# Expert lookups row by row, query products on unsplit weights, in a fused two-block kernel

## The chip, the cores and the metric

The kernel runs on one core of one Trainium2 chip. The metric is the device time of one execution in microseconds (us). One execution was also taken by the hardware profiler; its rows are used below. The engines are PE (TensorE: matmuls), DVE (VectorE), ACT (ScalarE), POOL (GpSimd) and SP (SyncE, which only issues transfers). Each runs its own instructions in program order and waits for the others by semaphores.

## What is computed

Two transformer blocks follow one another on 256 tokens of width 1024, in f32. The change lies in the second half of the first block, a layer that looks up experts (PEER), and at its border to the second block:

```python
h2 = modulate(x, norm_ffn_g, shift2, scale2)           # rmsnorm, scale, shift
q = (h2 @ w_q).reshape(T, 8, 2, 128)                   # 8 heads, two halves each
s = einsum('thpn', q, sub_keys)                        # 2 x 128 key scores
sv, si = top_k(s, 16)                                  # per half
cv, ci = top_k(all 16 x 16 sums of sv, 16)             # 16 of them
expert = si[half 0] * 128 + si[half 1] at ci           # 16 of 16384 experts
g = softmax(cv)
a = gelu(einsum('cd,chkd->chk', h2, u_tab[expert]))    # one row of 1024 each
y = einsum('chk,chkd->cd', g * a, v_tab[expert])
x = rmsnorm(x + gate2 * y, norm_final_g)               # then the second block
```

So each token takes 8 x 16 = 128 rows of `u_tab` and as many of `v_tab`, 4 KB each: 2 x 256 x 128 x 4 KB = 268 MB, all of it gathered from HBM by index.

## The kernel before

Tokens are worked on in two tiles of 128, one token to a partition. One gather (`gather`, L801) takes one expert row for each of the 128 tokens of a tile, 128 x 4 KB; `k` counts the 16 experts of one head. A unit is a tile and a head, 16 units in all, 8 of the first tile and then 8 of the second. For an expert row, DVE forms the dot product of `u` with the token's `h2` (L905, one value for each token, into a column of `act`). ACT applies Gelu (L930), DVE multiplies by the softmax weight (L931), ACT makes a diagonal matrix `dg` of the 128 weights (L916), and PE multiplies `dg` with `v` in two matmuls of 512 columns that add up in `acc` over the 128 rows of a tile (L919).

The loop (L869 to L937) goes by half units of eight rows. In half unit n it gathers and dots the u rows of this half and gathers and accumulates the v rows of the half before, one of each in turn; Gelu and weights come once for eight rows, behind the half. After the last half unit a round follows with eight v rows and no u rows. Each kind has three buffers of two rows (E, H, I for u; A, G, J for v). POOL issues every gather. Scores, top-k and the finish of the first tile are cut into steps (`Steps`, L88) that the loop runs between the rows: `more_queries` makes the queries and scores of heads 1 to 7, `next_topk` the expert numbers of the unit behind, `finish_tile` (L812) adds `x` and normalises, and its result is split for the second block.

Weight blocks (128 x 1024 f32) come through `Weights` (L28): a ring of seven raw buffers, and for blocks with `do_split` an ACT copy `hi` (L53) and a DVE difference `lo` (L54) in six buffers each. A product with such weights is three matmuls (`mm3`, L139 to L141) of hi and lo parts. The query weights `wq` are 16 blocks, two to a head. Four pairs of them are loaded into big buffers G, K, J, I ahead of time (`place`, L219), the others through the ring; all are split. The activations of the queries are split too (`xah`, `xal`, L635 and L638), scaled by A2 and still without the row's norm; the norm `rs` is multiplied into the product (L671) and the shift part `cq` added (L672). Before the loop stand the last output projection in four column blocks j (L625 to L640), head 0's queries for both tiles (L842 to L849), and the first steps of the first top-k; then six u gathers are issued (L859).

After the loop `band_values` (L948) starts the second block: its first products with `w_in_2`, for tile 0 between the finish steps of tile 1 and for tile 1 behind them.

## Time and profile before

| what | value |
|---|---|
| time, median of 3 runs | 1245.27 us (1242.26 to 1246.87) |
| profiled execution | 1246.47 us; span of its instructions 1244.7 us |
| PE busy | 1064.2 us, 86% of the span |
| DVE busy | 845.4 us, 68% |
| ACT busy | 462.0 us, 37% |
| POOL busy | 536.0 us, 43% |
| DMA | 390.59 MB, mean 314 GB/s |
| mean granted clock of TensorE | 0.983 |

Busy shares are means over stages with different limits. The page cuts the span into forty slices of 31 us and gives for each the busy tenths of the engines and of the DMA engines and the GB/s that they moved. The gathers run from about 222 to 890 us, slices 8 to 28. In these the DMA row reads 9 throughout and GB/s mostly 407 to 409, while PE reads 7 or 8. Before and behind them PE reads 9 nearly everywhere and DMA less.

### The profile page before, as it was taken

Reading aid. Unit: us, or ns where it says so; the run is one execution under the profiler, and the core shown is the slowest. Engines: PE = TensorE matmul, PEld = TensorE weight load, DVE = VectorE, ACT = ScalarE, POOL = GpSimd, SP = SyncE. Lnnn points to the kernel's source line nnn. Section 1 sums busy time; section 2 is a strip of 40 time slices with the busy share of each in tenths; the row PEclk is TensorE's granted clock in tenths of the full one; section 3 lists DMA queues with packets and bytes.
Section 4 is the critical chain, followed back from the end, with each engine's and each line's share of the span. In section 5 each row is a group of like instructions: output and inputs, shape, how many; then the busy total and the mean of one; then the engine's idle time right before and its main releaser. Section 6 shows DMA issues by size and latency. Waiting matters only on the chain.

```text
span 1244.7 us, 15745 instructions
## 1 busy us (share of the span) xinstructions
PE 1064.2 (86%) x5328; PEld 707.2 (57%) x5328; DVE 845.4 (68%) x1846; ACT 462.0 (37%) x887; POOL 536.0 (43%) x569
## 2 busy tenths in 40 slices
...
GB/s 346 330 315 307 321 284 153 278 346 406 409 386 392 407 408 409 409 409 409 358 409 409 409 409 409 409 409 409 347 289 185 153 186 123 197 181 194 183 123 34
DMA packets 161104, 390.59 MB, mean 314 GB/s; under 512 B 12472, under 2 KB 83648, under 8 KB 160768
## 3 DMA queue, kind: packets, MB, share of 16 engines
...
q10 hardware_dynamic: 640, 0.98, 0.2%
q14 instruction: 37, 0.30, 0.1%
HBM read 388.22 MB, written 1.06 MB: 313 GB/s over the span
## 4 chain that ended last, share of the span: by engine, by line
PE 37%; DMA 27%; DVE 12%; POOL 9%; issue 9%; ACT 4%; SPq 0%; DVEq 0%; POOLq 0%; ACTq 0%
DMA urows<-in_peer_u_dram,ex 19%; PE mm L139 7%; PE mm L141 7%; PE mm L140 7%; DMA vrows<-in_peer_v_dram,ex 5%; POOL vrows L806 5%; DVE dot L905 5%; POOL urows L806 5%; PE acc L919 3%; PE down L141 2%; PE down L139 2%; PE down L140 2%; DVE lo L54 1%; PE mp L407 1%; ACT hi L53 1%
## 5 line engine op out<-in xcount | busy, mean ns | idle before, releaser
L919 PE MATMUL acc<-vrows,dg 128*128 128x512 f32 x1024 | 491.5, 612 | 127.9 <-ACT dg L916 89.6
L905 DVE SCALAR_TENSOR_TENSOR dot<-urows,h2rows 128x1024 f32<-128x1024 f32 x256 | 312.0, 1219 | 173.7 <-DMA urows<-in_peer_u_dram,ex 172.3
L919 PEld LDWEIGHTS acc<-vrows,dg 128*128 128x128 f32 x1024 | 178.8, 190 | 420.7 <-issue 228.6
L806 POOL DMA_INDIRECT vrows<-in_peer_v_dram,ex x256 | 242.6, 948 | 103.8 <-issue 60.5
L806 POOL DMA_INDIRECT urows<-in_peer_u_dram,ex x256 | 241.7, 944 | 93.2 <-issue 65.4
L54 DVE TENSOR_TENSOR lo<-raw,hi 128x1024 fp32r<-128x1024 f32 (+1 forms) x152 | 182.0, 1222 | 89.6 <-ACT hi L53 88.0
L916 ACT ACTIVATE dg<-ident,wgt 128x128 f32<-128x128 f32 x256 | 96.0, 397 | 252.2 <-PE acc L919 246.7
L53 ACT CAST hi<-raw 128x1024 fp32r<-128x1024 f32 (+1 forms) x152 | 154.0, 1045 | 34.1 <-DMA raw<-in_w_in_dram 25.8
L139 PE MATMUL mm<-xh,hi 128*128 128x256 f32 x480 | 137.0, 285 | 2.2 <-ACT vab L1021 2.2
L140 PE MATMUL mm<-xl,hi 128*128 128x256 f32 x480 | 136.7, 285 | 0.0
L141 PE MATMUL mm<-xh,lo 128*128 128x256 f32 x480 | 135.6, 283 | 0.0
L139 PEld LDWEIGHTS mm<-xh,hi 128*128 128x128 f32 x480 | 91.1, 190 | 5.1 <-ACT vab L1021 2.5
L140 PEld LDWEIGHTS mm<-xl,hi 128*128 128x128 f32 x480 | 91.1, 190 | 0.4
L141 PEld LDWEIGHTS mm<-xh,lo 128*128 128x128 f32 x480 | 91.3, 190 | 0.0
L1120 POOL TENSOR_TENSOR r<-r,ln 128x512 f32<-128x512 f32 x2 | 3.0, 1488 | 195.2 <-ACT r L1119 195.2
L1176 DVE SCALAR_TENSOR_TENSOR u<-mm,col,u 128x255 f32<-128x255 f32 x88 | 42.4, 482 | 33.7 <-ACT u L1173 32.1
L337 POOL TENSOR_SCALAR p<-p,mnsm 128x128 f32<-128x128 f32 (+1 forms) x24 | 20.2, 851 | 91.1 <-DVE mnsm L335 79.2
L139 PE MATMUL mm<-hh,hi 128*128 128x256 f32 x160 | 47.6, 298 | 5.2 <-ACT hi L53 5.2
L852 POOL TENSOR_TENSOR h2T<-xT,rs 128x1024 f32<-128x1024 f32 x2 | 4.7, 2352 | 107.2 <-ACT rs L847 107.2
L1173 ACT ACTIVATE u<-mm,col 128x256 f32<-128x256 f32 x44 | 24.9, 566 | 59.1 <-PE mm L141 32.4
L141 PE MATMUL mm<-hh,lo 128*128 128x256 f32 x160 | 46.3, 289 | 0.5 <-DVE lo L54 0.5
L930 ACT ACTIVATE wgt<-act 128x8 f32<-128x8 f32 x32 | 6.6, 208 | 106.8 <-DVE dot L905 106.7
...
## 6 DMA issues: line engine op xcount, KB each, us to landing
...
urows<-in_peer_u_dram,ex POOLq DMA_INDIRECT x256, 8.0
```

Source lines behind the costliest of these rows:

```text
L53: self.nc.scalar.copy(hi, raw)
L54: self.nc.vector.tensor_tensor(lo, raw, hi.bitcast(F32), op=OP.subtract)
L139: nc.tensor.matmul(o, lh, rh, start=first, stop=False)
L140: nc.tensor.matmul(o, lh, rl, start=False, stop=False)
L141: nc.tensor.matmul(o, ll, rh, start=False, stop=last)
L337: eng.tensor_scalar(neg[:, s], neg[:, s], sm[:, i:i + 1], None, op0=OP.mult)
L806: nc.gpsimd.indirect_dma_start(out=g, out_offset=None, in_=tables[kind], in_offset=bass.IndirectOffsetOnAxis(ap=experts[unit][:, k:k + 1], ...
L905: nc.vector.scalar_tensor_tensor(dot, u, 1.0, h2rows, op0=OP.mult, op1=OP.mult, accum_out=act[:, half * HK + k:half * HK + k + 1])
L916: nc.scalar.activation(dg, ident, AF.Copy, scale=wgts[prev][:, k:k + 1])
L919: nc.tensor.matmul(acc[:, s], dg, v[:, s], start=prev == ((prev[0][0], 0), 0) and k == 0, stop=prev == ((prev[0][0], NH - 1), 1) and k == ...
L1173: nc.scalar.activation(dst, src, AF.Identity, bias=ccol[:, 3, c + f:c + f + 1], scale=ccol[:, 2, c + f:c + f + 1])
L1176: nc.vector.scalar_tensor_tensor(dst[:, n:], src[:, :256 - n], ccol[:, 2 - n, c + f:c + f + 1], dst[:, n:], op0=OP.mult, op1=OP.add)
```

## The change

Three things change together.

First, the query weights are no longer split. A query product is one f32 matmul (the chip works on it in four passes) with the raw block and with `xa`, a single f32 activation whose column 0 is the shift. All sixteen blocks are requested before the loop: seven through the ring, seven into the then unused `hi` and `lo` buffers (`borrow`), two into K.

Second, head 0 is done by token tile: `first_queries` makes tile 0's queries and scores alone, and tile 1's queries of head 0 come as the last of `more_queries`. Top-k of unit 0 reads the scores where PE left them.

Third, the loop goes row by row. A slot of 8 KB holds u and v of one expert row. There are seven slots for rows 0 to 111, and six from row 112 on, since D then serves the second block. In row s come the dot, Gelu, weight and `dg` of row s (`weigh`, three ACT instructions on one column, the last one the 128 x 128 diagonal), then PE's accumulation of row s - 1, then the gathers of u and v of row s + 6 (s + 5 from row 112 on). The finish of tile 0 runs every second row from row 129 on. Behind the loop, splits of `w_in_2` and products of `band_values` are interleaved with the finish of tile 1 in smaller parts.

```diff
+    def borrow(self, i, tag):
+        self.place(i, self.pool.tile([128, 1056], F32, tag=tag, name="whole", bufs=self.split_ahead))
...
-    def cols(key, w, c0, n):
...
-        cols(("wq", j), a["peer_wq"][0], j * 256, 256)
+        cols(("wq", j), a["peer_wq"][0], j * 256, 256, False)
     in2_order = [2568, 2824, 1544, 2056, 1800, 2312, 1280, 256, 768, 0, 512, 1024]
...
-    WQ_SLOTS = {"G": 4, "K": 14, "J": 6, "I": 2}
+    WQ_RING, WQ_K = 7, 14
     IN_SLOTS = {'A': [(0, 0), (0, 1)]}
-    ws.elsewhere = {wq_blocks[first + n] for first in WQ_SLOTS.values() for n in range(2)}
+    ws.elsewhere = set(wq_blocks[WQ_RING:])
     ws.elsewhere |= {W["in", j][g] for slot_blocks in IN_SLOTS.values() for j, g in slot_blocks}
...
             m.append(t)
         nc.vector.tensor_tensor(m[0], m[0], m[1], op=OP.add)
         split(mh[:, 2 * j:2 * j + 2, :], ml[:, 2 * j:2 * j + 2, :], m[0])
-        if j in (0, 2):
-            place("GK"[j // 2])
...
+    xa = big.tile([128, KC, 258], F32, tag="C", name="xa")
+    nc.vector.tensor_copy(xa[:, :, 0], shift2)
     sq_ps = aux_tile("sq_ps2")
     for j in range(4):
...
-            place("JI"[j])
         if j:
...
                                            modc[:, 16 + dc:17 + dc], xT[:, dc, :], op0=OP.mult, op1=OP.add)
-            nc.scalar.activation(xah[:, dc, 0:256], xT[:, dc, :], AF.Copy, scale=A2[:, dc:dc + 1])
...
         for dc in (2 * j, 2 * j + 1):
             nc.scalar.activation(sq2[:, dc, :], xT[:, dc, :], AF.Square)
-            nc.vector.scalar_tensor_tensor(xal[:, dc, 0:256], xT[:, dc, :], A2[:, dc:dc + 1],
-                                           xah[:, dc, 0:256].bitcast(F32),
-                                           op0=OP.mult, op1=OP.subtract)
+    for i in range(WQ_RING, WQ_K):
+        ws.borrow(wq_blocks[i], ("hi", "lo")[i % 2])
...
+    wq = {}
+    def wq_of(h):
+        if h not in wq:
+            wq[h] = [ws.get(i, 1) for i in W["wq", h]]
+        return wq[h]
+    def product(h, f, o, kcs, cs):
+        for kc in kcs:
+            nc.tensor.matmul(o, wq_of(h)[kc // 4][:, kc % 4, f * 128:(f + 1) * 128], xa[:, kc, cs],
+                             start=kc == 0, stop=kc == KC - 1)
...
+    cq0 = kp.tile([128, 2], F32, name="cq0", bufs=1)
+    def first_queries():
+        o = [mm_tile()[:, 0:129] for _ in range(2)]
+        for f in range(2):
+            product(0, f, o[f], range(0, 6), slice(0, 129))
+        square_sums(sq_ps, sq2, (6, 7))
+        for f in range(2):
+            product(0, f, o[f], (6, 7), slice(0, 129))
+        nc.scalar.copy(rs, rstd_rows(sq_ps, rstd))
+        qv = kp.tile([128, 512], F32, tag="qv", name="qv", bufs=1)
+        for f in range(2):
+            q = qv[:, f * 128:(f + 1) * 128]
+            nc.scalar.copy(cq0[:, f:f + 1], o[f][:, 0:1])
+            nc.vector.tensor_tensor(q, o[f][:, 1:129], rs[:, 0:128], op=OP.mult)
+            nc.vector.tensor_scalar(q, q, cq0[:, f:f + 1], None, op0=OP.add)
+        sp = aux_tile("sp")[:, 0:256]
+        key_scores(sp, 0, qv, 1, 128)
+        scores["first"] = sp.rearrange("p (a b) -> p a b", a=2)
...
     def queries(h):
...
+        n = 256 if h else 128
+        cs = slice(0, 257) if h else slice(129, 257)
+        o = [mm_tile()[:, 0:cs.stop - cs.start] for _ in range(2)]
+        for f in range(2):
+            product(h, f, o[f], range(0, KC // 2), cs)
+            if h:
+                yield
+            product(h, f, o[f], range(KC // 2, KC), cs)
+            yield
+        cq = kp.tile([128, 2], F32, tag="cq", name="cq") if h else cq0
         qv = kp.tile([128, 512], F32, tag="qv", name="qv", bufs=1)
...
+        for f in range(2):
+            q = qv[:, f * n:(f + 1) * n]
+            if h:
+                nc.scalar.copy(cq[:, f:f + 1], o[f][:, 0:1])
+            nc.vector.tensor_tensor(q, o[f][:, -n:], rs[:, 256 - n:], op=OP.mult)
             nc.scalar.activation(q, q, AF.Identity, bias=cq[:, f:f + 1])
...
+        sp = aux_tile("sp")[:, 0:2 * n]
+        key_scores(sp, h, qv, n // 128, n)
...
         scores[h] = kp.tile([128, 4, 128], F32, tag="scores", name="scores", bufs=8)
...
+        nc.scalar.copy(scores[h][:, 4 - n // 64:], sp.rearrange("p (a b) -> p a b", b=128))
         yield
...
-    def gather(kind, unit, k):
-        if k % 2 == 0:
...
-        g = rows[kind][:, k % 2, :]
...
+    row_tags = ["E", "H", "A", "I", "G", "J", "D"]
+    units = [(t, h) for t in range(2) for h in range(NH)]
+    N_ROWS = len(units) * K
+    SEVEN = 7 * K
+    rows = {}
...
+    def gather(s):
+        unit, k = units[s // K], s % K
+        r = slot(row_tags[s % 7 if s < SEVEN else (s - SEVEN) % 6], "uvrows")
+        for n, table in enumerate((a["peer_u"][0], a["peer_v"][0])):
+            nc.gpsimd.indirect_dma_start(out=r[:, n * 1024:(n + 1) * 1024], out_offset=None, in_=table,
+                                         in_offset=bass.IndirectOffsetOnAxis(ap=experts[unit][:, k:k + 1], axis=0))
+        rows[s] = r
...
+    first_queries()
...
-    ahead = [gather("u", (0, 0), k) for k in range(6)]
+    N_FIRST = 7
+    for s in range(N_FIRST):
+        gather(s)
...
+    more_queries = Steps(*(queries(h) for h in (*range(1, NH), 0)))
+    finish = Steps()
+    acc, dgs = None, {}
...
+        unit, k = units[s // K], s % K
+        c = slice(k, k + 1)
+        nc.scalar.activation(ge[:, c], act[:, c], AF.Gelu)
+        nc.scalar.activation(wgt[:, c], ge[:, c], AF.Copy, scale=gsm[unit][:, c])
+        dgs[s] = kp.tile([128, 128], F32, tag="dg", name="dg", bufs=3)
+        nc.scalar.activation(dgs[s], ident, AF.Copy, scale=wgt[:, c])
...
+    def accumulate(s):
+        t = units[s // K][0]
+        dg, v = dgs.pop(s), rows.pop(s)[:, 1024:2048]
+        for c in range(2):
+            cs = slice(c * 512, (c + 1) * 512)
+            nc.tensor.matmul(acc[:, cs], dg, v[:, cs], start=s % (N_ROWS // 2) == 0, stop=s % (N_ROWS // 2) == N_ROWS // 2 - 1)
+    next_row = N_FIRST
+    for s in range(N_ROWS):
+        n, k = s // K, s % K
...
+        if s == 6:
+            next_topk = Steps(topk(0, 1))
+        if n == 7 and k == 0:
+            more_queries.drain()
...
-        for k in range(HK):
-            if run:
-                u = ahead.pop(0) if ahead else gather("u", unit, half * HK + k)
-            if prev:
-                v = gather("v", prev[0], prev[1] * HK + k)
-            if run:
-                nc.vector.scalar_tensor_tensor(dot, u, 1.0, h2rows, op0=OP.mult, op1=OP.mult,
...
-                dg = kp.tile([128, 128], F32, tag="dg", name="dg", bufs=3)
-                nc.scalar.activation(dg, ident, AF.Copy, scale=wgts[prev][:, k:k + 1])
-                for c in range(2):
-                    s = slice(c * 512, (c + 1) * 512)
-                    nc.tensor.matmul(acc[:, s], dg, v[:, s], start=prev == ((prev[0][0], 0), 0) and k == 0,
-                                     stop=prev == ((prev[0][0], NH - 1), 1) and k == HK - 1)
-        if not run:
...
+        if s == N_ROWS // 2:
+            h2rows = h2rows_1
+        nc.vector.scalar_tensor_tensor(dot, rows[s][:, 0:1024], 1.0, h2rows, op0=OP.mult, op1=OP.mult,
+                                       accum_out=act[:, k:k + 1])
+        if s < 12 or k % 2:
+            more_queries.run()
+        next_topk.run(2 if n == 0 else 1)
+        if k % 2:
+            finish.run()
+        weigh(s)
+        if s:
+            if s - 1 in (0, N_ROWS // 2):
+                acc = pp.tile([128, 1024], F32, tag=("acc", "h2")[units[(s - 1) // K][0]], name="acc")
+            accumulate(s - 1)
+            if s == N_ROWS // 2:
+                xh, xl = slot3("C", "xh", KC, F32R), slot3("D", "xl", KC, F32R)
+                finish = Steps(finish_tile(0, acc))
+        if k == K - 5:
+            next_topk.drain()
+        last = next_row
+        while next_row < min(s + (7 if next_row < SEVEN else 6), N_ROWS):
+            gather(next_row)
+            next_row += 1
+        if last < next_row == N_ROWS:
             ws.limit, ws.queue = len(blocks), nc.gpsimd
             ws.prefetch()
             ws.queue = nc.sync
...
+    nc.scalar.activation(warm, eps_t[:, 0:1], AF.Sqrt)
+    accumulate(N_ROWS - 1)
...
-    ws.ensure(first_in2, first_in2 + 4)
...
...
+    def band_values(t, n, g):
...
     finish = Steps(finish_tile(1, acc))
     finish.run(2)
-    band_values(0)
+    ws.ensure(first_in2, first_in2 + 3)
+    for n, g in ((0, 0), (0, 1), (1, 0)):
+        band_values(0, n, g)
+    finish.run(2)
+    ws.ensure(first_in2, first_in2 + 4)
     finish.drain()
+    band_values(0, 1, 1)
     ws.ensure(first_in2, first_in2 + 6)
-    band_values(1)
+    for n in range(2):
+        for g in range(2):
+            band_values(1, n, g)
+            ws.parts.pop(vb_blocks[n][g])
```

How POOL's gathers stand against each other at the start of the loop, before (the last of the first six u gathers, then the loop; `ex` is the table of expert numbers, DMASW marks a gather done, DMAHW a plain transfer):

```order
L806 DMA urows_2401<-in_peer_u_dram,ex_2378 128x1024 [waits DMAHW5_49,DMAHW4_49]
L806 DMA urows_2401<-in_peer_u_dram,ex_2378 128x1024
L806 DMA urows_2503<-in_peer_u_dram,ex_2378 128x1024 [waits DMASW5_49,DMASW4_49,DVE_49]
L806 DMA urows_2503<-in_peer_u_dram,ex_2378 128x1024
L806 DMA urows_2585<-in_peer_u_dram,ex_2378 128x1024 [waits DMASW7_49,DMASW6_49,DVE_49]
L806 DMA vrows_2587<-in_peer_v_dram,ex_2378 128x1024 [waits DMAHW2_49]
L806 DMA urows_2585<-in_peer_u_dram,ex_2378 128x1024
L806 DMA vrows_2587<-in_peer_v_dram,ex_2378 128x1024
L806 DMA urows_2621<-in_peer_u_dram,ex_2378 128x1024 [waits DMASW1_49,DMASW0_49,DVE_49]
```

And now (the last of the first fourteen, then the loop):

```order
L826 DMA uvrows_2345<-in_peer_u_dram,ex_2313 128x1024 [waits DMASW6_49]
L826 DMA uvrows_2345<-in_peer_v_dram,ex_2313 128x1024 [waits DMASW7_49]
L826 DMA uvrows_2348<-in_peer_u_dram,ex_2313 128x1024 [waits DMASW0_49]
L826 DMA uvrows_2348<-in_peer_v_dram,ex_2313 128x1024 [waits DMASW1_49]
L826 DMA uvrows_2406<-in_peer_u_dram,ex_2313 128x1024 [waits DMASW2_49,DVE_49,PE_49]
L826 DMA uvrows_2406<-in_peer_v_dram,ex_2313 128x1024 [waits DMASW3_49]
L826 DMA uvrows_2420<-in_peer_u_dram,ex_2313 128x1024 [waits DMASW4_49,DVE_49,PE_49]
L826 DMA uvrows_2420<-in_peer_v_dram,ex_2313 128x1024 [waits DMASW5_49]
```

Before, u and v alternate, each with its own buffer, and a u buffer waits for DVE's dot. Now a row's u and v stand together, the u gather waits for DVE and PE, the v gather only for the transfer eight before it.

On DVE, from the last output projection (L633 before, L628 now) to the first top-k instruction, before:

```order
L54 TENSOR_TENSOR lo<-wqI,hi 128x1024 [waits DMAHW5_49,Activation_49]
L54 TENSOR_TENSOR lo<-wqG,hi 128x1024 [waits PE_49,Activation_49]
L633 SCALAR_TENSOR_TENSOR xT<-mm,modc,xT 128x256 [waits PE_49]
L633 SCALAR_TENSOR_TENSOR xT<-mm,modc,xT 128x256
L638 SCALAR_TENSOR_TENSOR xal<-xT,A_1961,xah 128x256 [waits Activation_49] x2
L313 RECIPROCAL rstd<-rstd 128x2 [waits Activation_49]
L671 TENSOR_TENSOR qv<-aux,rs 128x256 [waits Activation_49,Pool_49]
L671 TENSOR_TENSOR qv<-mm,rs 128x256 [waits Activation_49]
L703 MAX sv<-sp 128x8 [waits Activation_49]
```

And now:

```order
L628 SCALAR_TENSOR_TENSOR xT<-mm,modc,xT 128x256 [waits PE_49]
L628 SCALAR_TENSOR_TENSOR xT<-mm,modc,xT 128x256
L310 RECIPROCAL rstd<-rstd 128x2 [waits Activation_49]
L685 TENSOR_TENSOR qv<-mm,rs 128x128 [waits DVE_49,PE_49,Activation_49]
L686 TENSOR_SCALAR qv<-qv,cq_2244 128x128 [waits DVE_49]
L685 TENSOR_TENSOR qv<-mm,rs 128x128 [waits PE_49,Activation_49]
L686 TENSOR_SCALAR qv<-qv,cq_2244 128x128 [waits DVE_49]
L721 MAX sv<-sp 128x8 [waits PE_49]
```

The two lo splits ahead of the eviction, the lo part of the activations and the 256-column query steps are gone; four 128-column steps stand in front of top-k, and top-k waits for PE where it waited for ACT.

On DVE, from the last dot to the normalising of the second tile, before:

```order
L905 SCALAR_TENSOR_TENSOR dot,act<-urows,h2rows_4214 128x1024 [waits DMASW2_49,DVE_49]
L931 TENSOR_TENSOR wgt<-wgt,g 128x8 [waits Activation_49]
L54 TENSOR_TENSOR lo<-raw,hi 128x1024 [waits DMASW4_49,Activation_49]
L54 TENSOR_TENSOR lo<-raw,hi 128x1024 [waits DMASW5_49,Activation_49]
L819 TENSOR_TENSOR y_peer<-acc,gates 128x512 [waits PE_49]
L820 TENSOR_TENSOR y_peer<-y_peer,aux 128x512 [waits DVE_49,PE_49]
L819 TENSOR_TENSOR y_peer<-acc,gates 128x512
L820 TENSOR_TENSOR y_peer<-y_peer,aux 128x512 [waits DVE_49,PE_49]
L823 TENSOR_TENSOR st<-st 128x1 [waits Activation_49]
```

And now:

```order
L927 SCALAR_TENSOR_TENSOR dot,act<-uvrows,h2rows_4164 128x1024 [waits DMASW2_49,DVE_49]
L839 TENSOR_TENSOR y_peer<-acc,gates 128x512 [waits PE_49]
L840 TENSOR_TENSOR y_peer<-y_peer,aux 128x512 [waits DVE_49,PE_49]
L839 TENSOR_TENSOR y_peer<-acc,gates 128x512
L840 TENSOR_TENSOR y_peer<-y_peer,aux 128x512 [waits DVE_49,PE_49]
L54 TENSOR_TENSOR lo<-raw,hi 128x1024 [waits DMASW4_49,Activation_49]
L843 TENSOR_TENSOR st<-st 128x1
L846 RECIPROCAL st<-st 128x1 [waits Activation_49]
L849 SCALAR_TENSOR_TENSOR xin<-y_peer,st,gates 128x512 [waits DVE_49]
L849 SCALAR_TENSOR_TENSOR xin<-y_peer,st,gates 128x512
L54 TENSOR_TENSOR lo<-raw,hi 128x1024 [waits DMAHW1_49,DMASW5_49,Activation_49]
```

Before, the weights of eight rows and two lo splits of `w_in_2` stood between the last dot and `y_peer`. Now `y_peer` follows the last dot, one lo split stands between it and the sum `st`, and a second behind the normalised `xin`.

## Rows read from the trace of the kernel before

**Rows 1.** Busy us of each engine by stretch, granted clock, DMA rate.

```profile
core 0: us, PE busy (x) PEld busy (x) DVE busy (x) ACT busy (x) POOL busy (x), PEclk, DMA share, GB/s
218.00:230.00 12.00, 10.91 (x56) 8.76 (x56) 10.45 (x47) 5.35 (x13) 6.46 (x7) 0.72 0.44 137
230.00:270.00 40.00, 29.62 (x108) 18.95 (x109) 33.48 (x91) 13.78 (x27) 25.58 (x27) 0.83 0.91 341
340.00:400.00 60.00, 53.82 (x191) 29.02 (x190) 41.92 (x104) 19.11 (x42) 43.55 (x45) 1.00 1.00 388
560.00:640.00 80.00, 60.74 (x138) 23.24 (x136) 59.35 (x160) 21.39 (x49) 55.82 (x60) 0.98 0.99 389
640.00:880.00 240.00, 181.91 (x373) 63.76 (x372) 158.79 (x413) 52.25 (x125) 175.77 (x188) 0.99 1.03 409
218.00:890.00 672.00, 533.51 (x1426) 232.15 (x1427) 475.80 (x1267) 176.81 (x411) 480.30 (x508) 0.98 1.00 396
890.00:908.00 18.00, 17.16 (x43) 7.35 (x42) 1.48 (x4) 5.62 (x12) 10.05 (x12) 1.00 0.84 276
```

**Rows 2.** POOL's timeline: start, duration, engine, instruction, the idle time before it.

```profile
222.36 1.07 POOL L806 DMA_INDIRECT urows<-in_peer_u_dram,ex  x1 [3.71 <-DVE sp L710]
...
224.99 0.94 POOL L806 DMA_INDIRECT urows<-in_peer_u_dram,ex  x1 [0.30 <-issue]
...
255.79 0.94 POOL L806 DMA_INDIRECT vrows<-in_peer_v_dram,ex  x1 [4.62 <-PE acc L919]
...
598.32 1.09 POOL L806 DMA_INDIRECT vrows<-in_peer_v_dram,ex  x1 [5.13 <-PE acc L919]
```

**Rows 3.** From the page's DMA issues: the u gathers, median us to landing.

```profile
urows<-in_peer_u_dram,ex POOLq DMA_INDIRECT x256, 8.0
```

**Rows 4.** Timeline of all engines around the start of the gathers.

```profile
205.71 0.95 PE L307 MATMUL sq_ps<-ones,sq 128*128 128x1 f32 x8
...
207.06 1.22 DVE L54 TENSOR_TENSOR lo<-wqG,hi 128x1024 fp32r<-128x1024 f32 x1
...
208.20 0.87 DVE L633 SCALAR_TENSOR_TENSOR xT<-mm,modc,xT 128x256 f32<-128x256 f32 x2
...
208.71 0.91 ACT L635 ACTIVATE xah<-xT,A 128x256 fp32r<-128x256 f32 x2 [1.88 <-DVE xT L633]
...
212.88 0.60 PE L316 MATMUL sq_ps<-ident,rstd 128*128 128x128 f32 x4
...
213.52 0.37 ACT L847 COPY rs<-sq_ps 128x256 f32<-128x256 f32 x1 [1.74 <-PE sq_ps L316]
...
217.14 0.37 ACT L697 COPY scores<-sp 128x256 f32<-128x256 f32 x1 [1.02 <-PE sp L688]
...
217.55 0.50 DVE L703 MAX8 sv<-sp 128x8 f32<-128x128 f32 x2 [1.97 <-ACT scores L697]
...
227.92 1.22 DVE L905 SCALAR_TENSOR_TENSOR dot<-urows,h2rows 128x1024 f32<-128x1024 f32 x1
```

**Rows 5.** Timeline of all engines at the end of the gathers.

```profile
890.33 1.22 DVE L905 SCALAR_TENSOR_TENSOR dot<-urows,h2rows 128x1024 f32<-128x1024 f32 x1 [1.32 <-DMA urows<-in_peer_u_dram,ex]
...
891.61 1.96 PE L919 MATMUL acc<-vrows,dg 128*128 128x512 f32 x4 [0.56 <-DMA vrows<-in_peer_v_dram,ex]
...
893.85 13.97 PE L919 MATMUL acc<-vrows,dg 128*128 128x512 f32 x32 [0.28 <-DMA vrows<-in_peer_v_dram,ex]
...
907.92 1.23 DVE L54 TENSOR_TENSOR lo<-raw,hi 128x1024 fp32r<-128x1024 f32 x1 [15.92 <-ACT hi L53]
...
910.57 0.69 DVE L819 TENSOR_TENSOR y_peer<-acc,gates 128x512 f32<-128x512 f32 x1
```

**Rows 6.** ACT's timeline around a Gelu at the start of the gathers.

```profile
241.41 2.00 ACT L53 CAST hi<-wqJ 128x1024 fp32r<-128x1024 f32 x2
...
243.42 1.28 ACT L930 ACT_TABLE_LOAD   x1
...
244.72 0.21 ACT L930 ACTIVATE wgt<-act 128x8 f32<-128x8 f32 x1
...
246.40 0.40 ACT L916 ACTIVATE dg<-ident,wgt 128x128 f32<-128x128 f32 x1 [1.47 <-DVE wgt L931]
```

146 lines of the change are left out of this document (31 added, 115 removed).

## The prediction

> **What bounds the kernel now.** I read the page's forty slices first: from slice 8 to slice 28 the DMA row is 9, so the long middle, where expert rows are gathered, is bound by DMA traffic and not by an engine. The table of stretches says how well: 409 GB/s over 640 to 880 us with TensorE (PE) busy 182 of 240 us, DVE 159, POOL's gathers 176 [rows 1]. At 409 GB/s one gather of 128 rows of 4 KB (524,288 bytes) takes 1.282 us, a row pair (u and v) 2.564 us.
>
> The same table shows where the stream falls short: 341 GB/s over 230 to 270 (40 x 68/409 = 6.7 us lost), 388 over 340 to 400 (3.1), 389 over 560 to 640 (3.9), together 13.7 us [rows 1]. A check by bytes: 396 GB/s over 218 to 890 is 266.1 MB or 507.6 transfers, 650.7 us of full rate; by the 137 GB/s of the first stretch 3.1 transfers (4.0 us of full rate) were done at 230, so the stream ran from 226.0, and 890.0 - 226.0 - 650.7 = 13.3 us are lost. Then the POOL timeline: a gather takes 1.24 us of POOL (0.94, and 0.30 of idle time ahead), just under the DMA's 1.28; its long idles, 4.62 us at 255.79 and 5.13 us at 598.32, end on PE's accumulation, which frees a v slot [rows 2]. A gather lands 8.0 us after its issue in the median [rows 3].
>
> Last the two ends. At the start, DVE works on splits of query weights until 208.28 while the last output projection waits to be evicted at 208.20; top-k starts at 217.55, right behind a copy by ACT (217.14 + 0.37), and the first gather at 222.36, 4.81 us later [rows 2, 4]. At the end, the last u row is taken at 890.33, and eight rows of v alone follow in 13.97 us, 1.746 us each, PE without a gap: 907.82 [rows 5]. DMA needed only 1.282 us for each of them: 514 transfers (512 gathers, two w_in blocks that the ring loads in the stage) less 507.6 leave 6.4, so at full rate the traffic would have ended at 890.0 + 8.2 = 898.2.
>
> **The start.** The change takes wq splits off ACT and DVE. The last split's lo was in front of the eviction of out, j = 3. PE's matmuls end at about 205.9 (the square sums behind them start at 205.71), so xT moves from 208.20 to about 206.1, and xa is whole at 207.5. Then PE is late: square sums until 206.66 (205.71 + 0.95), 24 records of 129 columns, eight square sums (0.95), 8 more records, the row broadcast (0.60) [rows 4]. How long such an f32 record takes no row says. The nearest are the 128-column ones, four in 0.60 us with the tail of the last in it, so under 0.15 each [rows 4]; the far bound is a 512-column record, 13.97/32 = 0.437 [rows 5]. I take 0.125, near the first: 206.66 + 3.0 + 0.95 + 1.0 + 0.6 = 212.2, rs at 212.6 (before 213.89), four short DVE operations on 128 columns to 213.7, two key products to 214.3, top-k at 214.4, no longer behind ACT. That is 3.15 us earlier, and the first gather, 4.81 us behind, at 219.2. With 0.437 the 32 records would cost 10 us more, with 0.15 they cost 0.8 more, and at nothing at all the other side of the bound is 4 us less.
>
> All sixteen wq blocks are requested before that (ring, hi and lo buffers, K). The hi and lo buffers come free as the out blocks are used up, and DMA idles from about 206 until the first gathers, so I count their loading at nothing. If the cover failed, head 0 would not suffer, since its blocks are the first two in the ring.
>
> **The stream.** Same bytes, same number of gathers. What changes is when a slot comes free. Before, a u slot held two rows and fell free after the second dot, and POOL's next u and v alternate. Now one slot holds u and v of one expert row and falls free only after dot, Gelu, scale, dg and two matmuls. From u's landing: 1.22 + 0.08 (DVE), 0.21 + 0.21 + 0.40 (ACT; the Gelu row stands for the scale too), 1.96 (PE), four handoffs of 0.1: 4.5 us, or 3.2 after v's [rows 5, 6]. Slot cycle: 0.1 + 1.24 (u's issue) + 8.0 (v lands) + 3.2 = 12.6 us. Six slots at the DMA's pace give 6 x 2.564 = 15.4 us, seven 17.9. So DMA, not the slots, keeps setting the pace, with 2.8 us in hand, and 3.1 more before the queue is empty, because a landing takes 4.9 us in an empty queue (222.36 to 226.0 + 1.28) instead of 8.0.
>
> First rows: fourteen gathers keep POOL issuing for 17.4 us, to 236.6. Dot 0 follows top-k (227.92 before, so 224.8), dg 0 is out at about 227.3 with a table load, and the two matmuls take 1.96 us, or twice that at the lower of the two clock levels, of which the first stretch has much (0.72 granted): the first slot is free by 231.3, before POOL asks for it [rows 1, 4 to 6]. The stretch of 230 to 270, where 6.7 us were lost because v only began with the second half unit, should run at the full rate.
>
> PE in rows 12 to 95: a head's sixteen f32 products of 257 columns are 32 records; between 0.125 at 128 columns and 0.437 at 512 that is 0.23 each, 7.3 us, and 1.0 for keys, per 14 rows. With 14 x 1.746 it makes 32.7 of 35.9 us: it fits. Were a record 0.437, it would be 39.4, 3.5 us too much for each of six heads, 21 us: the far bound. The wq splits that were still done here leave DVE and ACT, which both have room in the stage (159 and 52 of 240 us), so I credit nothing for them [rows 1].
>
> Three places can still break the stream. Each unit has two ACT table loads, 2 x 1.28 in one row's release: covered by the 2.8. At row 112 the gate columns, two w_in splits and the transposes for the second token tile go in front of that row's dot; I sum ACT's and DVE's part to some 4.5 us of delay. From row 129 the finish of token tile 0 adds 5.5 us of DVE work over nine rows that also carry top-k. The last two are near the 5.9 us in hand. I take 3 us for them together; bounds are 0 and the 13.7 of before.
>
> So the stream starts at 226.0 - 3.15 = 222.85, 514 x 1.282 = 658.9, plus 3: the last v lands at 884.7.
>
> **The end.** The accumulation ends 3.2 us later, at 887.9, against 907.82: 19.9 us earlier. Behind it, two lo splits stood in front of y_peer (907.92 to 910.57, 2.7 us) [rows 5]; now one stands between y_peer and the norm and one between the norm and xl, and each waits for ACT's hi. The first is ACT 1.05 and DVE 1.23 in series, so I count the finish at zero, with -2.7 and +2.7 as its bounds. The seven w_in blocks that POOL issues behind the last gathers land in their order, 1.28 us apiece, the two needed first before 887.9. After that PE is busy throughout, and the rest moves as one.
>
> Sum: -3.15 (start) -13.3 + 3 (stream) -9.6 + 3.2 (end: 907.82 - 898.2 against 3.2), in all -19.9. The profiled run took 1246.47 us, its span 1244.70; so 1226.6 for a like run. The profiled run lies 1.2 over the median of 1245.27, so I predict 1225.4, own range 1217 to 1234.
>
> **Rivals.**
> 1. The breaks stay. Slots now wait for PE, as the two longest idles of POOL did before [rows 2]; against it speaks that those came where PE had fallen behind by whole rows. If all 13.3 us are lost again, -19.9 + 10.3 = -9.6, 1235.7.
> 2. A table switch costs more than its load. Mechanism: twice per unit the Gelu of one row waits for both switches. The rows show a load of 1.28, the instruction before it ending at 243.41 and the next starting at 244.72, so nothing beyond it [rows 6]. The Trainium skill, "ScalarE: Activation LUTs", section "What ACT_TABLE_LOAD costs", gives 1283 ns and a drain of about 1380 ns on top for every switch to another set; this trace agrees with the first and shows no place for the second. As a mechanism in rows: if a switch cost twice its 1.28, that row's cycle would be 12.6 + 5.1 = 17.7 against 15.4, 2.3 us lost in each of nine units, 20.7 us: 1246, no change.
> 3. Slower: the slot cycle becomes the bound in rows 112 to 255. Place: POOL's wait for the accumulation with six slots. Price: above 15.4 us each further us of cycle costs 144/6 = 24 us. For it: dot stands behind top-k steps on DVE, the ACT chain is in series, PE in order. Against: it needs 2.8 us more on every row, where the three-instruction ACT chain is 0.82 long and PE has a quarter of its time free. It cancels the gain at 16.2 us; at 17 us the time is 1225 + 38 = 1263.
>
> **How the numbers follow.** Chances: forecast 0.72, rival 1 0.14, rival 2 0.05, rival 3 0.09. About 0.5% (6.2 us) is what a measurement of this kernel can tell from no change. Faster than 1239.0 by forecast and rival 1: 0.86; same 0.06; slower than 1251.5 0.08. The range: below, no breaks (-3), the finish at -2.7 and a start 1 us better give 1218.7, and with the spread of the runs 1216; above, rival 1 with the finish at +2.7 gives 1238.4, so 1239. Left out are rivals 2 and 3 and little else.
>
> **What would show it.** First gather near 219 and DMA at 409 GB/s from 230 on: the start and the first rows are right. Breaks, if any, at rows 112 and 128 to 140. POOL's gathers then wait for transfers and not for acc. Last dot near 884, acc ended near 888, no run of v rows alone. Wrong, if the median stretch of the stage lies under 400 GB/s with POOL waiting for PE each row, or if PE has no gaps before row 100.

## The result, and the profile after

The changed kernel takes 1233.27 us (median of 5, 1231.6 to 1235.5), the kernel before 1245.27 us (median of 5). The ratio is 0.9905, 95% interval 0.9889 to 0.9921: 12.0 us faster. The forecast was 1225.4 us with a range of 1216 to 1239, so the sign and the range held (also the narrower 1217 to 1234 that the prediction names first); of the 19.9 us that the sum gave, 12 came. The time lies nearer to the 1235.7 of rival 1, "the breaks stay", than to the forecast, so it takes the trace to tell the two apart. The profiled execution took 1234.79 us, its span 1233.0.

The stretches of the changed kernel, to be laid beside [rows 1] (busy us of each engine, granted clock, DMA share, GB/s):

```profile
218.00:230.00 12.00, 7.87 (x26) 6.36 (x26) 9.99 (x45) 4.97 (x11) 5.39 (x6) 0.72 0.27 80
230.00:270.00 40.00, 34.35 (x106) 19.82 (x107) 27.33 (x77) 19.05 (x56) 29.17 (x32) 0.96 1.02 398
340.00:400.00 60.00, 57.55 (x168) 31.51 (x167) 39.24 (x99) 27.54 (x85) 42.36 (x46) 0.96 1.02 410
500.00:560.00 60.00, 48.94 (x116) 20.55 (x115) 39.16 (x98) 30.42 (x83) 40.67 (x44) 0.91 0.99 383
560.00:640.00 80.00, 62.58 (x139) 24.73 (x140) 59.70 (x158) 37.62 (x109) 58.78 (x63) 0.96 1.03 409
640.00:880.00 240.00, 186.81 (x374) 66.74 (x372) 157.36 (x401) 98.14 (x301) 176.22 (x188) 0.97 1.02 408
```

The three stretches that were short before, 341, 388 and 389 GB/s, are at 398, 410 and 409. A new one has come in, 383 over 500 to 560 us (60 x 26/409 = 3.8 us), and the first stretch has only 80 GB/s in place of 137: the gathers start later, not earlier.

The start, all engines, from the square sums behind the last output projection to the first gather (compare [rows 4]):

```profile
207.81 0.95 PE L304 MATMUL sq_ps<-ones,sq 128*128 128x1 f32 x8
...
208.99 2.92 PE L659 MATMUL mm<-xa,raw 128*128 128x129 f32 x24 [0.23 <-issue]
...
214.63 4.64 POOL L865 TENSOR_TENSOR h2T<-xT,rs 128x1024 f32<-128x1024 f32 x2 [105.78 <-ACT cq L684]
214.64 0.29 DVE L685 TENSOR_TENSOR qv<-mm,rs 128x128 f32<-128x128 f32 x1 [1.45 <-ACT cq L684]
214.97 2.08 DVE L686 TENSOR_SCALAR qv<-qv,cq 128x128 f32<-128x128 f32 x1
216.97 0.28 DVE L685 TENSOR_TENSOR qv<-mm,rs 128x128 f32<-128x128 f32 x1
...
217.29 2.07 DVE L686 TENSOR_SCALAR qv<-qv,cq 128x128 f32<-128x128 f32 x1
...
220.24 0.50 DVE L721 MAX8 sv<-sp 128x8 f32<-128x128 f32 x2 [0.89 <-PE sp L666]
...
224.66 1.07 POOL L826 DMA_INDIRECT uvrows<-in_peer_u_dram,ex  x1 [5.39 <-DVE sp L728]
```

Two additions on 128 columns take 2.07 and 2.08 us, seven times the multiplications beside them. Both end some 0.1 us behind one of POOL's two instructions (214.63 + 2.32 = 216.95, and 219.27).

The end, all engines (compare [rows 5]): the issue of the last u row, the last dot, the last accumulation, `y_peer`, and the first lo split.

```profile
884.02 0.94 POOL L826 DMA_INDIRECT uvrows<-in_peer_u_dram,ex  x1 [0.30 <-issue]
...
893.45 1.22 DVE L927 SCALAR_TENSOR_TENSOR dot<-uvrows,h2rows 128x1024 f32<-128x1024 f32 x1 [1.34 <-DMA uvrows<-in_peer_u_dram,ex]
...
895.73 1.98 PE L896 MATMUL acc<-uvrows,dg 128*128 128x512 f32 x4 [0.58 <-ACT dg L889]
...
897.75 0.69 DVE L839 TENSOR_TENSOR y_peer<-acc,gates 128x512 f32<-128x512 f32 x1 [3.07 <-PE acc L896]
...
902.35 1.23 DVE L54 TENSOR_TENSOR lo<-raw,hi 128x1024 fp32r<-128x1024 f32 x1 [1.72 <-ACT hi L53]
```

The run of eight v rows is gone; 4.3 us behind the last dot the sum is complete. Span against span (us):

| piece | before | after | difference | forecast |
|---|---|---|---|---|
| up to the square sums of j = 3 | 205.71 | 207.81 | +2.1 | 0 |
| from there to the first gather | 16.65 | 16.85 | +0.2 | -3.15 |
| first gather to the end of `acc` | 685.46 | 673.05 | -12.4 | -16.75 |
| from there to the eviction of the first `w_in` products | 17.30 | 17.08 | -0.2 | 0 |
| the rest of the span | 319.58 | 318.21 | -1.4 | 0 |

The first and the last piece are taken for the scatter of an execution: the same 2.1 us stand between the two traces from 162 us on, where nothing is changed, and a second profile of the changed kernel has these square sums at 206.09. Without these two pieces the profiles differ by 12.4 us, the medians by 12.0. So two of the forecast's terms were too good, the start by 3.35 us and the stream by 4.35.

### The profile page after: what moved, and what is told of

Its sections match the earlier page's. It is cut to its first block, busy times and chain, and to the rows that moved or that the text cites. A ratio compares the mean times of both kernels' runs of the same rounds, so it can differ in the third digit from the quotient of the medians.

```text
span 1233.0 us, 16011 instructions
## 1 busy us (share of the span) xinstructions
PE 1073.8 (87%) x5232; PEld 716.1 (58%) x5232; DVE 824.7 (67%) x1793; ACT 574.8 (47%) x1350; POOL 533.5 (43%) x569
## 4 chain that ended last, share of the span: by engine, by line
PE 42%; DMA 22%; POOL 11%; DVE 10%; issue 9%; ACT 5%; SPq 0%; ACTq 0%; POOLq 0%; DVEq 0%
DMA uvrows<-in_peer_u_dram,ex 20%; POOL uvrows L826 11%; PE mm L143 8%; PE mm L145 7%; PE mm L144 7%; PE acc L896 6%; DVE dot L927 3%; PE down L145 2%; PE down L143 2%; PE down L144 2%; PE mm L659 1%; PE mp L404 1%; ACT p L328 1%; ACT hi L53 1%; PE yp L370 1%
## 5 line engine op out<-in xcount | busy, mean ns | idle before, releaser
L896 PE MATMUL acc<-uvrows,dg 128*128 128x512 f32 x1024 | 501.2, 627 | 112.8 <-ACT dg L889 107.4
L927 DVE SCALAR_TENSOR_TENSOR dot<-uvrows,h2rows 128x1024 f32<-128x1024 f32 x256 | 311.8, 1218 | 192.6 <-DMA uvrows<-in_peer_u_dram,ex 191.2
L896 PEld LDWEIGHTS acc<-uvrows,dg 128*128 128x128 f32 x1024 | 188.2, 196 | 397.4 <-ACT dg L889 227.5
L826 POOL DMA_INDIRECT uvrows<-in_peer_u_dram,ex x256 | 241.0, 941 | 107.3 <-issue 64.4
L826 POOL DMA_INDIRECT uvrows<-in_peer_v_dram,ex x256 | 240.4, 939 | 78.2 <-issue 68.6
L54 DVE TENSOR_TENSOR lo<-raw,hi 128x1024 fp32r<-128x1024 f32 x144 | 172.6, 1222 | 79.2 <-ACT hi L53 78.5
L886 ACT ACTIVATE ge<-act 128x1 f32<-128x1 f32 x256 | 51.5, 201 | 321.1 <-DVE dot L927 320.7
L53 ACT CAST hi<-raw 128x1024 fp32r<-128x1024 f32 x144 | 146.1, 1045 | 31.6 <-DMA raw<-in_w_in_dram 23.8
L889 ACT ACTIVATE dg<-ident,wgt 128x128 f32<-128x128 f32 x256 | 102.8, 401 | 8.4
L887 ACT ACTIVATE wgt<-ge,g 128x1 f32<-128x1 f32 x256 | 75.4, 295 | 8.3
```

Source lines behind the costliest of these rows:

```text
L53: self.nc.scalar.copy(hi, raw)
L54: self.nc.vector.tensor_tensor(lo, raw, hi.bitcast(F32), op=OP.subtract)
L826: nc.gpsimd.indirect_dma_start(out=r[:, n * 1024:(n + 1) * 1024], out_offset=None, in_=table, in_offset=bass.IndirectOffsetOnAxis(ap=exper ...
L886: nc.scalar.activation(ge[:, c], act[:, c], AF.Gelu)
L887: nc.scalar.activation(wgt[:, c], ge[:, c], AF.Copy, scale=gsm[unit][:, c])
L889: nc.scalar.activation(dgs[s], ident, AF.Copy, scale=wgt[:, c])
```

## The experiments

The runs came in three groups, each on a chip of its own. On the first group's chip the kernel before took 1328.0 us and the gathers some 363 GB/s; its times are given as ratios to that, and mostly its traces are used. In the second and third group the kernel before took 1243.8 and 1244.6 us. The changed kernel was run again in the second group alone, so a difference from it in the other groups rests on two chips. Each ratio is to the kernel before on the same chip, with its 95% interval.

**The shift on ACT.** The two additions go to ACT, where the kernel before had them.

```diff
-            nc.vector.tensor_scalar(q, q, cq0[:, f:f + 1], None, op0=OP.add)
+            nc.scalar.activation(q, q, AF.Identity, bias=cq0[:, f:f + 1])
```

> The two DVE additions of the query shift (128x128, 2.08 us each, in front of top-k) are made by ACT instead. Theory A, DVE stood still there because POOL's product h2T <- xT, rs (214.63 to 219.27) held what the addition needs: on ACT they take some 0.3 us each, top-k and the first gather come 3.2 to 3.6 us earlier, first gather about 21.2 us behind the last square sums instead of 12.0 + ... that is at about 221.2 of a span like the changed kernel's (224.66 there), and the time falls from 1233.3 to about 1229.8. Theory B, such an addition with a scalar per partition is slow by itself: the same gain, so this run doesn't part A from B; the two runs beside it do. Theory C, the stream of gathers makes up for a late start elsewhere: no gain, 1233.

Measured: 0.40 us each, first gather 8.0 us behind the first query multiplication (213.61 to 221.60) in place of 10.0. Ratio 0.995 (0.991 to 0.999), 1317.3 us; the changed kernel itself was not in this group, so the time does not tell theory C from the others. In the trace 2.0 us came of the 3.2 to 3.6: top-k began 3.3 us earlier relative to that multiplication, but its first part took longer (from the first MAX8 to the second 5.50 us, in the changed kernel 4.19). One row holds that, an addition of 64 columns with both inputs in SBUF, which ends at 218.34, right behind POOL's two instructions (213.60 + 4.66 = 218.26), and took 0.20 us in the changed kernel:

```profile
213.60 4.66 POOL L865 TENSOR_TENSOR h2T<-xT,rs 128x1024 f32<-128x1024 f32 x2 [105.78 <-ACT cq L684]
...
216.82 1.52 DVE L745 TENSOR_TENSOR cand<-sv 128x64 f32<-128x64 f32 x1
```

**POOL's product in pieces.**

```diff
-    for g in range(2):
-        ks = slice(4 * g, 4 * g + 4)
-        nc.gpsimd.tensor_tensor(h2T[:, ks], xT[:, ks], rs[:, None, :].to_broadcast([128, 4, 256]), op=OP.mult)
+    for kc in range(KC):
+        nc.gpsimd.tensor_tensor(h2T[:, kc, :], xT[:, kc, :], rs, op=OP.mult)
```

> POOL's product h2T in eight instructions of 128x256 (about 0.59 us each) instead of two of 2.32 us; the DVE additions stay on DVE. Theory A (the addition waits for the POOL instruction under way to end): each addition falls from 2.08 us to at most 0.3 + 0.6 = 0.9 us and ends where a POOL instruction ends. Theory B (slow by itself): 2.08 us as before.

One execution (1317.0 us), used for its trace alone. Its timeline of POOL and DVE:

```profile
215.71 5.51 POOL L864 TENSOR_TENSOR h2T<-xT,rs 128x256 f32<-128x256 f32 x8 [107.36 <-ACT cq L684]
215.72 0.29 DVE L685 TENSOR_TENSOR qv<-mm,rs 128x128 f32<-128x128 f32 x1 [1.45 <-ACT cq L684]
216.05 0.47 DVE L686 TENSOR_SCALAR qv<-qv,cq 128x128 f32<-128x128 f32 x1
216.44 0.28 DVE L685 TENSOR_TENSOR qv<-mm,rs 128x128 f32<-128x128 f32 x1
...
216.75 0.45 DVE L686 TENSOR_SCALAR qv<-qv,cq 128x128 f32<-128x128 f32 x1
```

The same addition on DVE takes 0.47 and 0.45 us: it is not slow by itself, and it ends some 0.1 us behind the first and the second of POOL's eight (0.69 us each: 216.40 and 217.09). Theory B falls.

**The addition with two SBUF inputs.**

```diff
+            nc.vector.tensor_tensor(q, q, cq0[:, f:f + 1].to_broadcast([128, 128]), op=OP.add)
```

> The same additions on DVE as a tensor-tensor addition with the scalar column broadcast, so with two SBUF inputs; POOL's product as in the changed kernel. If only the fast mode of the tensor-scalar form needs what POOL holds: 0.28 us each, as the multiplication next to it that reads PSUM (0.29). If any second input from SBUF needs it, as the Trainium skill (SBUF - State Buffer, on the shared port pair) has it: about 2 us each again, ending with POOL's instructions. If slow by the scalar operand: 0.28.

Again one execution (1318.3 us), used for its trace alone.

```profile
213.54 4.70 POOL L865 TENSOR_TENSOR h2T<-xT,rs 128x1024 f32<-128x1024 f32 x2 [105.97 <-ACT cq L684]
213.55 0.29 DVE L685 TENSOR_TENSOR qv<-mm,rs 128x128 f32<-128x128 f32 x1 [1.45 <-ACT cq L684]
213.88 2.15 DVE L686 TENSOR_TENSOR qv<-qv,cq 128x128 f32<-128x128 f32 x1
...
216.26 2.12 DVE L686 TENSOR_TENSOR qv<-qv,cq 128x128 f32<-128x128 f32 x1
```

A tensor-tensor addition out of SBUF waits as long (2.15 and 2.12 us); the multiplication, with one input in PSUM, does not (0.29). So it is not the form of the instruction alone: what waits has all its inputs in SBUF. The Trainium skill, "SBUF — State Buffer", section "Who interferes with whom", says that a DVE instruction with two SBUF inputs, or in a two-port mode, and a GpSimd instruction that reads SBUF lock each other out for a whole instruction; these three runs agree, with 2.07 to 2.15 against 0.29 us.

**POOL's product left out**, on top of the shift on ACT (the activation then reads `xT`).

```diff
-        nc.gpsimd.tensor_tensor(h2T[:, ks], xT[:, ks], rs[:, None, :].to_broadcast([128, 4, 256]), op=OP.mult)
-        nc.scalar.activation(h2T[:, kc, :], h2T[:, kc, :], AF.Identity, bias=shift2[:, kc:kc + 1], scale=A2[:, kc:kc + 1])
+        nc.scalar.activation(h2T[:, kc, :], xT[:, kc, :], AF.Identity, bias=shift2[:, kc:kc + 1], scale=A2[:, kc:kc + 1])
```

> The shift on ACT, and POOL's product of h2T with the row's norm left out (h2 then lacks the norm). It shows what POOL still costs the top-k behind it: with the product on POOL and the shift on ACT the first MAX8 and the second stood 5.5 to 5.6 us apart, with POOL done 4.2. Theory A, DVE operations with two SBUF inputs wait for POOL in the first top-k too: 4.2 us apart again, and the first gather 6.7 us behind the first query multiplication in place of 8.0. Theory B, ACT or PE delays it: 5.5 us as it was.

One execution, 1228.3 us.

```profile
215.97 0.50 DVE L721 MAX8 sv<-sp 128x8 f32<-128x128 f32 x2 [1.22 <-PE sp L666]
...
216.91 0.21 DVE L745 TENSOR_TENSOR cand<-sv 128x64 f32<-128x64 f32 x1
...
220.16 0.50 DVE L721 MAX8 sv<-sp 128x8 f32<-128x128 f32 x2
...
220.53 1.07 POOL L826 DMA_INDIRECT uvrows<-in_peer_u_dram,ex  x1 [112.74 <-PE h2rows L813]
```

The `cand` addition is back at 0.21 us, from MAX8 to MAX8 it is 4.19 us again, and the first gather 6.87 us behind the multiplication at 213.66. From the square sums behind the last output projection (206.83) it is 13.7 us, and the forecast had 13.5. So POOL's product accounts for what the start lacked: 2.0 us by the two additions, 1.1 by top-k once they are off DVE.

**The changed kernel again**, for the second group.

> The changed kernel once more, as it is, beside the others of this group: its time and its stages are what they are read against. First gather some 10.0 us behind the first query multiplication of DVE (214.64 to 224.66 in the first profile), 0.99 of the kernel before.

1232.98 us, ratio 0.992 (0.9895 to 0.9946). Square sums 206.09, first gather 222.94 (16.85 us behind them again), `acc` complete at 896.1 (673.2 behind the first gather). So these pieces repeat within 0.1 us.

**The old order of lookups.** Everything as changed, only the loop, `gather` and its buffers are those of the kernel before; the query steps run in each of the first sixteen rows, where the kernel before ran them in the first eight and then in every second.

```diff
-    row_tags = ["E", "H", "A", "I", "G", "J", "D"]
+    tags = {"u": ["E", "H", "I"], "v": ["A", "G", "J"]}
...
-    for s in range(N_ROWS):
+    for n, run in enumerate(runs + [None]):
...
+            if n < 2 or k % 2:
+                more_queries.run()
```

> The changed kernel (unsplit query weights, head 0 by token tile, the new order behind the loop), but with the lookups of the kernel before: half units of eight rows, u and v a half unit apart, three buffers of two rows for each. It isolates the third part of the change. By the prediction's ledger the lookups row by row brought the whole gain (in the profiles 12.4 us from the first gather to the end of the accumulation, and the start nothing): about 1233.3 + 12 = 1245, with the run of eight v rows (some 14 us, PE without a gap) back at the end. Rival: the relief of PE and DVE by the unsplit weights closed the breaks at 230 to 270 and 340 to 400 us (6.7 and 3.1 us lost in the kernel before), and the order of lookups brought only the tail: about 1233.3 + 6.5 = 1240.

> The changed kernel with the lookups of the kernel before (half units of eight rows, u and v apart, three buffers of two rows each), once more, beside the changed kernel on the same chip. Theory A, the lookups row by row bring the gain (from the first gather to the end of the accumulation 685.5 us before, 673.1 after): 6 to 12 us slower than the changed kernel. Theory B, the unsplit query weights bring it, by giving PE, DVE and ACT room in the first hundred rows: within 2 us of the changed kernel or faster, with the run of eight v rows still at the end.

In the second group 1238.07 us, ratio 0.9955 (0.9938 to 0.9972): 5.7 us under the kernel before, 5.1 over the changed one. So the rest of the change brings half of the gain and the lookups row by row the other half: of the first expectation the rival's 1240 comes nearer, of the second neither theory fits. The traces agree: both first gathers stand 16.8 us behind the square sums, and from there to the end of `acc` it is 678.2 us here against 673.2. On the slower chip of the first group it took 1309.8 us (0.987, 0.980 to 0.995), below the shift on ACT with lookups row by row (0.995, 0.991 to 0.999); the two intervals overlap, so whether the order turns round there stays open. The stretches of its trace in the second group:

```profile
230.00:270.00 40.00, 30.66 (x103) 19.48 (x104) 34.10 (x104) 11.84 (x28) 27.01 (x29) 0.87 1.03 402
340.00:400.00 60.00, 55.24 (x159) 28.83 (x158) 42.26 (x121) 16.70 (x42) 44.04 (x47) 0.97 1.03 409
500.00:560.00 60.00, 45.60 (x101) 16.49 (x100) 42.51 (x115) 15.23 (x33) 43.36 (x47) 1.00 1.03 410
560.00:640.00 80.00, 60.43 (x137) 23.06 (x136) 56.46 (x145) 21.54 (x50) 55.50 (x60) 0.98 0.98 386
```

and its end on DVE and PE:

```profile
883.50 1.22 DVE L917 SCALAR_TENSOR_TENSOR dot<-urows,h2rows 128x1024 f32<-128x1024 f32 x1 [1.28 <-DMA urows<-in_peer_u_dram,ex]
...
884.78 16.04 PE L929 MATMUL acc<-vrows,dg 128*128 128x512 f32 x36 [0.56 <-DMA vrows<-in_peer_v_dram,ex]
```

With u and v half a unit apart as before, the first two short stretches are nearly whole, 402 and 409 GB/s where there were 341 and 388. Only the third, 386, and the tail of v rows stay.

**Six slots throughout.**

```diff
-    SEVEN = 7 * K
+    SEVEN = 0
-    N_FIRST = 7
+    N_FIRST = 6
```

> The changed kernel with six slots for all 256 rows and six rows gathered ahead. Theory of the prediction, a slot is free again 12.6 us after its u gather is asked for, six slots at the pace of the DMA give 15.4: no loss over most rows, at most 2 us from the first hundred rows, where PE is 94% busy; within 2 us of the changed kernel. Rival, PE holds the slots in the first hundred rows: 5 us or more slower, with POOL waiting for the accumulation there.

1234.73 us, ratio 0.993 (0.991 to 0.995): 1.8 us over the changed kernel, within the 2 us expected but hardly above the scatter. From the first gather to the end of `acc` it is 2.1 us more (675.3 against 673.2).

**Five slots throughout**, the same edit with 5.

> Five slots for all rows, five rows gathered ahead. In the changed kernel a slot's cycle, from the issue of its u to the end of its accumulation, was 13.7 us (884.02 to 897.71), of which 9.3 to the landing of u. Five slots at the pace of the DMA give 5 x 2.564 = 12.8. Theory A, the landing is mostly waiting behind other transfers and shrinks with fewer of them: no more than some 8 us slower than with six slots, most of it in the first hundred rows. Theory B (the slot cycle as the bound, the slower rival of the prediction), the landing keeps its length: 0.9 us lost in each five rows, 45 us slower.

1251.01 us, ratio 1.005 (1.003 to 1.007): by the ratios 15 us, by the times 16 us slower than six slots, between the two theories. One line of each, six slots and then five, 640 to 880 us (the profiled execution with five, 1255.38 us, was the longest of its five):

```profile
640.00:880.00 240.00, 183.72 (x372) 65.06 (x370) 156.93 (x401) 97.85 (x299) 175.37 (x188) 0.99 1.03 408
```

```profile
640.00:880.00 240.00, 181.91 (x365) 65.77 (x364) 156.65 (x407) 98.86 (x298) 171.01 (x182) 0.97 1.01 398
```

398 in place of 408 is 0.06 us a row, not the 0.18 of theory B: the landing of a u row took 6.8 us in the median, against 8.0 with six slots, so it shortens, as theory A has it. With five slots the cycle begins to bind, and the breaks cost more (357 against 382 over 500 to 560 us, 375 against 407 over 560 to 640).

**Head 0 for both tiles ahead of the loop**, with the shift on ACT.

```diff
-            product(0, f, o[f], range(0, 6), slice(0, 129))
+            product(0, f, o[f], range(0, 6), slice(0, 257))
```

> The changed kernel with head 0's queries for both token tiles ahead of the loop again (32 records of 257 columns in place of 129), the shift on ACT as in the kernel before. A record of 257 columns took 0.218 us in the loop, one of 129 columns 0.115 to 0.122 ahead of it: 32 x 0.1 = 3.3 us more in front of the norm. The shift on ACT gives 2 us back. First gather 1 to 2 us later against the first query's place, time 0 to 2 us over the changed kernel. Rival: PE is not what top-k waits for there; then 2 us under the changed kernel.

1230.89 us, ratio 0.9879 (0.9857 to 0.9902): 2.1 to 2.4 us under the changed kernel of the other groups, where 0 to 2 over were expected; the ratios' intervals overlap, so the pieces of the trace say more. The start came as worked out, the first gather 18.2 us behind the square sums (205.40 to 223.59) in place of 16.85, 1.34 later, so PE is waited for. But the stretch from there to the end of `acc` was 2.4 us shorter (670.8 against 673.2), so the two pieces together are 1.0 us under the changed kernel; the rest of the 2.1 to 2.4 lies in pieces that the edit does not touch. SP's row of the two `w_in` blocks, in this kernel and then in the changed one, shows what I had not thought of:

```profile
211.19 3.87 SPq L73 DMA_DIRECT2D raw<-in_w_in_dram  x2
```

```profile
237.90 3.82 SPq L73 DMA_DIRECT2D raw<-in_w_in_dram  x2
```

Here the two blocks are loaded ahead of the first gather, while DMA has little else to do (131 GB/s over 211 to 219 us, and 0 in the changed kernel); there they come in among the first rows and take two transfers' time, 2 x 1.282 = 2.56 us. That would account for the 2.4; it was not tried by itself.

**Three edits together.** The shift on ACT; the work ahead of row 112 spread over rows 98 to 114; seven slots up to row 125.

```diff
-    SEVEN = 7 * K
+    SEVEN = 126
...
-        if n == 7 and k == 0:
-            more_queries.drain()
...
+        if s in (98, 100, 102, 104):
+            dst, src, c = prepare.pop(0)
...
+        if s in (108, 110):
+            ws.ensure(first_in2, first_in2 + (s - 106) // 2)
...
+        if s in (112, 114):
+            token_rows(h2rows_1[:, (s - 112) * 256:(s - 110) * 256], h2T, 1, (s - 112) * 2, 4)
```

> The changed kernel with three edits: the query shift of head 0 on ACT; the block in front of row 112 spread over rows 98 to 114 (gate columns one piece each second row, the two splits of w_in at rows 108 and 110, where DVE has no top-k, the transposes of the second tile at rows 112 and 114); seven slots up to row 125. The first brings the first gather 2 us forward (8.0 us behind the query multiplication in place of 10.0); the others take away the two breaks in the stream at 505 and 528 us (by 2.564 us a row the dots fell back there by 2.2 us in all). Expected 3 to 4 us under the changed kernel. Rival: the stream catches up anyway since transfers are queued, then only the 2 us of the start.

1229.32 us, ratio 0.9892 (0.987 to 0.9915): 3.7 under the changed kernel, as expected. The first gather stands 14.8 us behind the square sums, 2.0 less, and from there to the end of `acc` it is 671.2 us, 1.9 less. The break at 500 to 560 is gone, and a new one stands where the step to six slots now meets the finish of tile 0:

```profile
500.00:560.00 60.00, 49.35 (x109) 19.71 (x109) 39.93 (x97) 26.27 (x79) 44.31 (x47) 0.94 1.02 409
566.00:586.00 20.00, 17.91 (x43) 8.16 (x44) 17.13 (x46) 13.20 (x32) 12.38 (x14) 0.85 0.96 349
```

**The finish of tile 0 later**, on top of these.

```diff
-        if k % 2:
+        if k > K - 6:
             finish.run()
```

> The three edits of the run before (query shift of head 0 on ACT; the work ahead of row 112 spread over rows 98 to 114; seven slots up to row 125), and the finish of tile 0 moved from rows 129, 131, ... to rows 139 to 143, where DVE has no top-k. In the run before, the step from seven to six slots had met the finish of tile 0: 349 GB/s over 566 to 586 us, 2.9 us lost. If these two made that break together, it goes, and the time is 1.5 to 3 us below the run before, about 0.987 of the kernel before. Rival: the step from seven to six slots alone makes it, since one row is asked for later; then no change.

1229.38 us, ratio 0.9875 (0.985 to 0.990). The times are equal and the intervals of the two ratios overlap; the start is 14.8 us again, and from the first gather to the end of `acc` it is 672.0 us against 671.2. So the gain expected did not come. The break did go from 566 to 586 us, so the step to six slots alone does not make it, but another stands at 600 to 620, where the finish now ends:

```profile
566.00:586.00 20.00, 13.13 (x28) 4.38 (x27) 15.24 (x43) 9.80 (x28) 15.12 (x17) 1.00 1.03 409
600.00:610.00 10.00, 9.93 (x25) 4.78 (x25) 6.69 (x25) 4.26 (x13) 4.99 (x7) 0.83 0.97 360
610.00:620.00 10.00, 8.40 (x19) 3.17 (x18) 9.79 (x28) 3.60 (x12) 7.56 (x9) 1.00 0.97 362
```

These 20 us lose 2.4 us (10 x 49/409 + 10 x 47/409), about as much as the break that went (2.9).

## Why the prediction was right, and where its terms were off

**The bound.** Right: the gathers set the pace, 398 to 412 GB/s in every stretch from 230 us on but the one with the break at 500 to 560, and the slots don't: six would do (1.8 us more), five would not (15 to 16 more). The slower rival (slot cycle) needed more than 15.4 us a cycle; the last rows show 13.7 (u issued at 884.02, accumulated at 897.71), 1.1 more than the 12.6 worked out. Rival 1 (the breaks stay) is out by its places, since the three old breaks closed, but not by its size: 7.35 us of the stream stayed lost, between the 3 of the forecast and the 13.3 of the rival. Of the signs that the prediction named, the rate from 230 us on and the missing run of v rows came; the first gather (224.66 for 219), the last dot (893.45 for 884) and the end of `acc` (897.71 for 888) came late. That the time still fell into the range owes something to rival 1 having been counted into it. The rival of the table switch is out: two loads stand between three dots at the full pace,

```profile
501.37 1.28 ACT L803 ACT_TABLE_LOAD   x1
501.64 1.22 DVE L927 SCALAR_TENSOR_TENSOR dot<-uvrows,h2rows 128x1024 f32<-128x1024 f32 x1
...
503.26 0.19 ACT L803 ACTIVATION_READ_ACCUMULATOR g<-cv,ng 128x1 f32 x1
503.46 1.28 ACT L886 ACT_TABLE_LOAD   x1
...
504.23 1.22 DVE L927 SCALAR_TENSOR_TENSOR dot<-uvrows,h2rows 128x1024 f32<-128x1024 f32 x1 [1.22 <-DMA uvrows<-in_peer_u_dram,ex]
504.75 0.20 ACT L886 ACTIVATE ge<-act 128x1 f32<-128x1 f32 x1
...
506.71 1.22 DVE L927 SCALAR_TENSOR_TENSOR dot<-uvrows,h2rows 128x1024 f32<-128x1024 f32 x1 [0.90 <-DMA uvrows<-in_peer_u_dram,ex]
```

and the second load is over with its 1.28 us: the instruction before it ends at 503.45, the next starts at 504.75. The drain that the Trainium skill, "ScalarE: Activation LUTs", section "What ACT_TABLE_LOAD costs", puts on top of it has no place here either.

**The start** (-3.15 forecast, +0.2 measured). PE's part held: 24 records in 2.92 us are 0.122 each, 0.125 were taken. The step that failed is "four short DVE operations on 128 columns to 213.7". They took 4.7 us where 1.1 were counted, since POOL starts its product in the same moment and two of the four have all their inputs in SBUF. The kernel before had these additions on ACT, so its trace showed no such wait. With POOL's product left out, the forecast of the start is met within 0.2 us.

**The stream** (4.35 us short). Row 13 was dotted 43.1 us behind the first gather (267.76 - 224.66); by the sum it was 3.65 + 29 x 1.282 = 40.8, the two `w_in` blocks included, so 2.3 us were lost by then. The sum had the full rate from 228.3 on (3.65 us behind the first gather); DMA moved 221, 252, 336, 317 and 373 GB/s in the five stretches of 2 us from 226 on. Counted in bytes, this slow beginning costs little: at 236 us 5.7 transfers were moved, and the sum has 6.0, since transfers began before 228.3. At the dot of row 14 (270.26 us), which needs 31 transfers landed, 32.4 had been moved. So others were under way beside the one waited for, where the sum let them land one behind the other; that this makes the 2.3 us is argued, not tried.

From row 13 to row 255 it was 625.7 us; 242 x 2.564 and the 3 us for breaks make 623.5, 2.2 short. The two places that the 3 us were for took less: the dot of row 112 comes 7.93 us behind the one before it, of which 5.4 are late and some 2.3 stay late, and the finish of tile 0 cost nothing that lasted.

```profile
519.38 1.22 DVE L927 SCALAR_TENSOR_TENSOR dot<-uvrows,h2rows 128x1024 f32<-128x1024 f32 x1 [1.26 <-DMA uvrows<-in_peer_u_dram,ex]
...
527.31 1.21 DVE L927 SCALAR_TENSOR_TENSOR dot<-uvrows,h2rows 128x1024 f32<-128x1024 f32 x1
```

What the forecast lacked came later, in places that it did not name: against a pace of 2.564 us the dots fell back 1.4 us between rows 144 and 152 and 1.6 between rows 208 and 240, and 1.2 and 1.4 there in the second profile of the changed kernel. No run shows what makes them.

**The cause of the old breaks** was told wrongly, though the sum did not suffer. The forecast put the 6.7 us of 230 to 270 on v, which only began with the second half unit, and credited nothing for the splits taken off DVE and ACT. With the old order of lookups and the new queries this stretch is nearly whole (402 GB/s). So the rest of the change closes the first two breaks (some 9 of 13.7 us), and the row order closes the third and does away with the tail, though it opens the one at row 112. That it is the splits within that rest (and not head 0 by token tile or the other spread of the query steps) was not tried apart. From the last dot to the end of `acc` it is 17.3 us with the old order (883.50 to 900.82) and 4.3 with the new.

**The finish** was costed at nothing and measured at -0.2 us.
